# Four-head score groups, earlier-free accumulators in the opening, and moved value products in a two-layer decoder trunk

## The chip, the cores and the metric

The kernel runs on one core of one Trainium2 chip. The metric is the device time of one execution in microseconds (us); lower is better. Matrix products run on TensorE (PE in the profile), elementwise work on VectorE (DVE) and ScalarE (ACT), small powers on GpSimd (POOL); SyncE (SP) issues the loads. A weight load of TensorE is PEld.

## The reference, cut to what matters

A sequence of 256 positions of width 1024 goes through two layers. Layer A is a dilated sliding-window attention: three groups (window, dilation) = (128,1), (512,4), (2048,16), each with its own q, k and v of 16 heads of 64, merged by their softmax denominators. Layer B is causal attention over one block of 256. Each layer is followed by a gated ConvFFN of inner width 2816. All is float32.

```python
def reference(x, ...):
    for i in range(2):
        hn = rmsnorm(x, attn_norm[i])
        x = x + (mixer_dilated if i == 0 else mixer_moba)(hn, ...)   # qkv, q/k norm, rope, softmax, w_o
        hn = rmsnorm(x, ffn_norm[i])
        x = x + conv_ffn(hn, ffn_w_up[i], ffn_conv_w[i], ffn_conv_b[i], ffn_w_down[i])
    return x
```

## The kernel before, in words

Every weight matrix is streamed from HBM in units of 512 KB to 1 MB (`Stream`). ScalarE rounds a unit to its high part (`whi`, line 103), VectorE subtracts to get the low part (`wlo`, line 111), and TensorE makes each product from three multiplications (high by high, low by high, high by low; lines 428 to 430, 485 and 843 to 845).

The whole program is written out by hand as a sequence of turns. `turn` starts some weight units on ScalarE, runs what was put down for this turn in the list `first`, finishes one weight unit, runs the list `pre`, finishes the other units, issues a piece of a product on TensorE, and last runs the list `post`. Every engine works in the order in which the instructions are issued there. `at(post, 2, f)` puts f into the list of two turns later. In `post` the order is `step_C`, `step_A`, `step_T`, `transpose` (while the turn number is under 80).

Layer A works in four sections of four heads. A section's turns each hold 12 products of 512 columns. A section has four products for q and k of the three groups and for v (and in sections 0 and 2 one more for v), so it has 20, 16, 20 and 16 turns. After a q/k product come: squares and a copy out of the accumulator on ScalarE (lines 502, 503), sums and rotation on VectorE (`head_sums`, 508 to 520), a power on POOL, a scaling (`factors`, 530), and four TensorE transposes (`transpose`, 545), whose copies are lines 575 and 581 to 583. In the section's turn 14 and later the softmax steps follow, for one chunk of 128 queries (c) and some heads at a time:

- `step_A` (TensorE): scores of two heads side by side, three pairs of 64-row products with 256 columns (645), then for the dilated groups 16 products of 64 x 64 (654).
- `step_E` (VectorE, ScalarE): mask, maximum, exponential (667 to 677); `step_R`: division by the sum (684, 687).
- `step_T` (TensorE): transposes of the probabilities (694); `step_V` (ScalarE): copies out of PSUM (701).
- `step_C` (TensorE): value products, for all four heads and both chunks at once (725), and then `split_T` (416, 417).

PLANS gives the turns at which the groups of two heads stand in even and odd sections; a turn past the section's end falls into the next section. PSUM has eight banks: three for `acc`, two for `S`, two for `PT`, one for `O`. A pool gives out the buffer whose last use stands earliest in the program, and the first writer waits for that last use.

In section 0 the products of groups 0 and 1 (`both_chunks`) take one weight unit per turn and work on both chunks. `out_proj` is the output projection in pieces, each one weight unit by one chunk; OUT_ORDER gives their order. Layer B's mixer has the same steps with other sizes.

Of the kernel before, what the change touches and what calls it, by code (L numbers as in the profile page):

```python
# [44 lines left out]

PLANS = (14, 18, 24, 26), (14, 16, 22, 24)

# [88 lines left out]
def trunk_kernel(ctx, tc, x, a_w_qkv, a_w_o, b_w_qkv, b_w_o, ffn_norm, ffn_w_up, ffn_w_down, pack, mask_a, mask_b,  # L136
# [196 lines left out]
    class LateNorm(Norm):  # L333
# [20 lines left out]
        def transpose(self, h):  # L354
            xg = bp.tile([P, 512], F32, name="qk", bufs=4)
            t = self.flip(xr[:, self.c, h * 512:(h + 1) * 512], ("S", "PT")[self.c], 2)
            g = self.gain[:, h * 4:h * 4 + 4, None].to_broadcast([P, 4, P])
            nc.vector.tensor_mul(xg.rearrange("p (k t) -> p k t", t=P), t.rearrange("p (k t) -> p k t", t=P), g)
            split_T(self.dst, h * 4, 4, self.c, xg)

    class FirstNorm:
# [21 lines left out]
        def sums(self):  # L383
            acc = ps.tile([P, 512], F32, name="S", bufs=2)
# [48 lines left out]
    def attention(xT, norms, ng, g0, mask):  # L433
# [62 lines left out]
        def qk_block(sec, g, res, rq):  # L496
# [27 lines left out]
            def factors(c, qk, rs):  # L524

                h0 = 0 if dil else HS
                if not dil:
                    rq[c] = rs
                t3 = qk.rearrange("p (h d) -> p h d", d=HD)[:, h0:]
                nc.vector.tensor_mul(t3, t3, rs[:, h0:, None].to_broadcast([P, 8 - h0, HD]))  # L530
                at(post, 1, transpose, c, qk)

            def transpose(c, qk):
                if c == 0:
# [8 lines left out]
                tp = ps.tile([P, 512], F32, name="S", bufs=2) if dil and sec == 0 and g < 2 else new_acc()  # L543
                for i in range(4):
# [39 lines left out]

            yield from both_chunks(done) if dil and sec == 0 and g < 2 else product(done)

# [38 lines left out]

        O, weights = {}, {}

        def step_A(sec, c, heads, qkT, v, rq):

            S2 = [ps.tile([P, 512], F32, name="S", bufs=2) for _ in range(2)]  # L630
            n = 3 * P if dil else (c + 1) * P
            cs = slice(c * P, (c + 1) * P)

            for i in range(0, len(heads), 2):
                two = [(S2[h % 2], i // 2 * n, slice(h % 2 * HD, h % 2 * HD + HD), h // 2) for h in heads[i:i + 2]]
                if not dil and c == 0:
# [10 lines left out]
                if dil:  # L647
                    for a in range(2):
                        r = slice(a * 64, (a + 1) * 64)
                        for j in range(2):  # L650
                            t = qkT[1 + (a + j) % 2][c]
                            for s2, o, rows, pr in two:
                                oj = o + S + j * 64
                                nc.tensor.matmul(s2[r, oj:oj + 64], r32(t[rows, 0, pr, r]), r32(t[rows, 1, pr, r]),
                                                 start=True, stop=True)
            at(first, 1, step_E, sec, c, heads, v, rq, S2, n)

        def step_E(sec, c, heads, v, rq, S2, n):
            den = sp.tile([P, 4], F32, name="den", bufs=2)
            sm = bp.tile([P, 768], F32, name="sm", bufs=2)  # L660
            mx = sp.tile([P, 4], F32, name="mx", bufs=2)
            nb_ = sp.tile([P, 4], F32, name="nbias", bufs=2)

            m = len(heads)
            for i, h in enumerate(heads):
                o = i // 2 * n
                nc.vector.tensor_tensor_reduce(
                    out=sm[:, i * n:(i + 1) * n], in0=S2[h % 2][:, o:o + n], in1=mask[:, c * moff:c * moff + n],
                    op0=ALU.add, op1=ALU.max, scale=1.0, scalar=-3.0e38, accum_out=mx[:, i:i + 1])
            if dil:  # L670
                nc.vector.tensor_scalar_mul(nb_[:, 0:m], mx[:, 0:m], -1.0)
            else:
                f = rq[c][:, heads[0]:heads[0] + m]
                nc.vector.scalar_tensor_tensor(nb_[:, 0:m], mx[:, 0:m], -1.0, f, op0=ALU.mult, op1=ALU.mult)
            for i, h in enumerate(heads):
                sl = slice(i * n, (i + 1) * n)
                nc.scalar.activation(sm[:, sl], sm[:, sl], AF.Exp, bias=nb_[:, i:i + 1],
                                     scale=1.0 if dil else rq[c][:, h:h + 1], accum_out=den[:, i:i + 1])
            at(first, 1, step_R, heads, sm, den, n)
            at(post, 1 if dil or sec < NSEC - 1 else 2, step_T, sec, c, heads, v, sm, n)  # L680

        def step_R(heads, sm, den, n):
            rd = sp.tile([P, 4], F32, name="rd", bufs=2)
            nc.vector.reciprocal(rd[:, 0:len(heads)], den[:, 0:len(heads)])
            for i in range(len(heads)):
                sl = slice(i * n, (i + 1) * n)
                nc.vector.tensor_scalar(sm[:, sl], sm[:, sl], rd[:, i:i + 1], None, op0=ALU.mult)

        def step_T(sec, c, heads, v, sm, n):
            tot = n * len(heads)  # L690
            Tp = [ps.tile([P, 512], F32, name="PT", bufs=2) for _ in range((tot + 511) // 512)]
            for b in range(tot // P):
                o = b % 4 * P
                nc.tensor.transpose(Tp[b // 4][:, o:o + P], sm[:, b * P:(b + 1) * P], ident)  # L694
            at(pre, 1, step_V, sec, c, heads, v, Tp, tot)

        def step_V(sec, c, heads, v, Tp, tot):
            pT = bp.tile([P, 768], F32, name="pT", bufs=4)
            for i, t in enumerate(Tp):
                w = min(512, tot - i * 512)  # L700
                nc.scalar.activation(pT[:, i * 512:i * 512 + w], t[:, 0:w], AF.Copy)

# [3 lines left out]
            if heads[-1] < HS - 1 and (whole or not dil) or whole and c == 0:  # L706
                weights[key] = held
            else:
                at(post, 1, step_C, sec, held)

        def step_C(sec, held):

            for c, heads, pT, v in held:
# [4 lines left out]
                for i in range(0, len(heads), 2):  # L718
# [3 lines left out]
                    for n, (b, q, vb) in enumerate(blocks):  # L722
                        for j, h in enumerate(heads[i:i + 2]):
                            o, p = h // 2 * P, ((i + j) * nblk + b) * P
                            nc.tensor.matmul(O[sec, c][j * HD:(j + 1) * HD, c, o + q.start:o + q.stop],  # L725
                                             vb[:, h * HD:(h + 1) * HD], pT[:, p + q.start:p + q.stop],
                                             start=(n == 0), stop=(n == len(blocks) - 1))
# [10 lines left out]
        for sec in range(NSEC):  # L738
            qk, v, rq = [], vs[sec], {}
            for s, c, heads in last if sec == NSEC - 1 else odd if sec % 2 else plan:  # L740
                at(post, s, step_A, sec, c, heads, qk, v, rq)
# [9 lines left out]
    def out_proj(l, aT, dst):  # L751
# [4 lines left out]
        def piece(*idx):  # L756
            def go():
                for c, i in idx:
# [4 lines left out]
                    if u == 0:  # L763
                        acc[c, n] = ps.tile([P, 512], F32, name="S" if c and n else "acc", bufs=2 if c and n else 3)
                    for kk in range(2):
# [22 lines left out]
    def ffn(xT, l, end):  # L788
# [4 lines left out]

        st0 = [{"acc": ps.tile([P, 512], F32, name="PT", bufs=2)} for _ in range(2)]
        box = {}
# [103 lines left out]
        def down(b, c, ns=(0, 1), piece=None):  # L899
            f, e = divmod(b, 2)  # L900
            cs = slice(e * S + c * P, e * S + (c + 1) * P)
            if not dacc:
                dacc.extend([ps.tile([P, 512], F32, name=t, bufs=2) for _ in range(2)] for t in ("S", "PT"))
            if b not in dw:
# [69 lines left out]

    warm = ps.tile([P, 512], F32, name="PT", bufs=2)
    nc.scalar.activation(sp.tile([P, 512], F32, name="sq", bufs=2)[:, 0:P], ident, AF.Copy)
# [129 lines left out]
```

## Time and profile before

| | |
|---|---|
| median of 3 runs | 775.03 us (774.76 to 775.91) |
| the profiled execution: its time, its span | 775.08 us, 773.3 us |
| TensorE busy | 767.4 us (99%) |
| weight loads busy | 641.7 us (83%) |
| VectorE busy | 575.3 us (74%) |
| ScalarE busy | 497.5 us (64%) |
| HBM traffic | 172 GB/s over the span |

The span is the time from the first to the last instruction in the profile. The busy time of TensorE counts pipelined products whose ends are modelled, so that 99% busy does not say that each product takes as little time as it could; the distance from one start to the next does.

### The profile page before, as it was taken

To read this page: it belongs to the slowest core of one execution; us is meant where nothing else is said; L and a number is where in the kernel's file an instruction comes from. 1 tells how busy PE (TensorE), PEld (TensorE's weight loads), DVE (VectorE), ACT (ScalarE), POOL (GpSimd) and SP (SyncE) were. 2 spreads that over 40 slices of the span, in tenths; PEclk is the share of its full clock that TensorE was granted. 3 is DMA by queue.
4 is the path that set the end of the run, shared out by engine and by line. 5 is a ranking of instruction groups with operands and counts; after the bars stand their busy time and mean duration, and the time that the engine had idled before them with its cause. 6 is when DMAs were issued, how large, how long until landed. Compare 5 with 4: busy or idle time off the path is not lost.

```text
span 773.3 us, 12315 instructions
## 1 busy us (share of the span) xinstructions
PE 767.4 (99%) x4532; PEld 641.7 (83%) x4532; DVE 575.3 (74%) x1075; ACT 497.5 (64%) x867; POOL 84.1 (11%) x109
## 2 busy tenths in 40 slices
PE   8999999999999999999999999999999999999998
PEld 7878888888887789988888888787778988888886
DVE  6966767765786566878787786978866788877874
ACT  7768567567657556565666656868765566576560
POOL 1530331420232000000000002123000000000000
PEclk9999999999999999999999999999999999999999
DMA  9966536455546426556666563743526456656631
GB/s 285 326 189 182 156 110 191 137 164 164 158 151 207 141 81 206 177 183 198 195 208 197 166 217 107 231 151 109 183 90 201 153 181 197 212 172 190 197 103 54
DMA packets 108060, 133.84 MB, mean 173 GB/s; under 512 B 5856, under 2 KB 92768, under 8 KB 108000
## 3 DMA queue, kind: packets, MB, share of 16 engines
q1 hardware_dynamic: 107424, 130.96, 53.7%
q0 software_dynamic: 576, 2.10, 0.8%
q8 instruction: 35, 0.57, 0.3%
q14 instruction: 25, 0.20, 0.1%
HBM read 131.99 MB, written 1.05 MB: 172 GB/s over the span
## 4 chain that ended last, share of the span: by engine, by line
PE 92%; DVE 3%; ACT 1%; DMA 1%; issue 1%; SPq 0%; DVEq 0%; ACTq 0%
PE acc L428 12%; PE acc L430 12%; PE acc L429 12%; PE acc L843 12%; PE acc L845 6%; PE O L843 4%; PE S L909 3%; PE S L911 3%; PE S L910 3%; PE PT L909 3%; PE PT L911 3%; PE PT L910 3%; PE PT L694 2%; PE O L725 2%; PE acc L868 2%; PE acc L866 2%
## 5 line engine op out<-in xcount | busy, mean ns | idle before, releaser
L111 DVE TENSOR_TENSOR wlo<-raw,whi 128x1024 fp32r<-128x1024 f32 x240 | 287.7, 1220 | 6.5 <-ACT whi L103 6.3
L103 ACT ACTIVATE whi<-raw 128x1024 fp32r<-128x1024 f32 x240 | 244.9, 1053 | 5.1 <-DMA raw<-in_a_w_qkv_dram 2.2
L428 PE MATMUL acc<-whi,xT 128*128 128x512 f32 x432 | 175.2, 406 | 0.0
L430 PE MATMUL acc<-wlo,xT 128*128 128x512 f32 x432 | 169.0, 391 | 0.0
L429 PE MATMUL acc<-whi,xT 128*128 128x512 f32 x432 | 168.5, 390 | 0.1
L843 PE MATMUL acc<-xT,whi 128*128 128x512 f32 x384 | 137.3, 398 | 0.0
L845 PE MATMUL acc<-xT,wlo 128*128 128x256 f32 x384 | 107.8, 281 | 0.0
L430 PEld LDWEIGHTS acc<-wlo,xT 128*128 128x128 f32 x432 | 81.1, 188 | 17.9
L428 PEld LDWEIGHTS acc<-whi,xT 128*128 128x128 f32 x432 | 81.2, 188 | 16.5 <-issue 1.2
L429 PEld LDWEIGHTS acc<-whi,xT 128*128 128x128 f32 x432 | 81.4, 188 | 15.5 <-DVE xT L417 0.5
L843 PEld LDWEIGHTS acc<-xT,whi 128*128 128x128 f32 x384 | 72.1, 188 | 17.5
L845 PEld LDWEIGHTS acc<-xT,wlo 128*128 128x128 f32 x384 | 72.4, 189 | 1.2
L883 DVE SCALAR_TENSOR_TENSOR qk<-sm,pk,qk 128x254 f32<-128x254 f32 (+1 forms) x128 | 54.6, 478 | 4.0 <-ACT qk L880 3.1
L292 POOL TENSOR_TENSOR rs_y<-rs_v,mhalf 128x8 f32<-128x8 f32 x32 | 54.6, 1705 | 2.7
L855 DVE TENSOR_TENSOR sm<-acc,pT 128x256 f32<-128x256 f32 x48 | 20.3, 423 | 36.4 <-ACT pT L854 36.4
L880 ACT ACTIVATE qk<-sm,pk 128x256 f32<-128x256 f32 x64 | 38.3, 598 | 13.3 <-DVE sm L855 13.2
L843 PE MATMUL O<-xT,whi 128*128 128x512 f32 x128 | 46.1, 399 | 0.0
L892 ACT ACTIVATE kT<-qk 128x512 fp32r<-128x512 f32 x22 | 13.9, 633 | 47.7 <-DVE qk L890 47.7
L886 ACT ACTIVATE qk<-qk 128x512 f32<-128x512 f32 x22 | 13.9, 634 | 41.9 <-DVE qk L883 41.9
L290 POOL TENSOR_SCALAR rs_v<-qssq,rn_e 128x8 f32<-128x8 f32 x32 | 14.3, 446 | 212.8 <-DVE qssq L508 212.8
L866 PE MATMUL acc<-xT,whi 128*128 128x256 f32 x128 | 36.4, 284 | 0.0
L868 PE MATMUL acc<-xT,wlo 128*128 128x256 f32 x128 | 36.2, 283 | 0.0
(174 smaller groups left out, 1258.1 us busy)
## 6 DMA issues: line engine op xcount, KB each, us to landing
raw<-in_ffn_w_up_dram SPq DMA_DIRECT2D x80, 512.0 KB, 4.6
raw<-in_a_w_qkv_dram SPq DMA_DIRECT2D x144, 256.0 KB, 4.3
raw<-in_ffn_w_down_dram SPq DMA_DIRECT2D x44, 512.0 KB, 3.3
raw<-in_b_w_qkv_dram SPq DMA_DIRECT2D x48, 256.0 KB, 3.7
raw<-in_a_w_o_dram SPq DMA_DIRECT2D x8, 512.0 KB, 4.0
raw<-in_ffn_w_up_dram SPq DMA_DIRECT2D x16, 256.0 KB, 4.5
raw<-in_b_w_o_dram SPq DMA_DIRECT2D x8, 512.0 KB, 4.0
xr<-in_x_dram POOLq DMA_DIRECT2D x2, 512.0 KB, 6.0
```

Of the source, the lines that this page charges most:

```text
L103: self.nc.scalar.activation(hi, raw, AF.Copy)
L111: self.nc.vector.tensor_sub(lo, self.raw[self.done], r32(hi))
L292: nc.gpsimd.tensor_tensor(y, v, mhalf[:, 0:n], op=ALU.pow)
L428: nc.tensor.matmul(acc, T[:, k, 0, cs], hi, start=first, stop=False)
L429: nc.tensor.matmul(acc, T[:, k, 1, cs], hi, start=False, stop=False)
L430: nc.tensor.matmul(acc, T[:, k, 0, cs], lo, start=False, stop=last)
L843: nc.tensor.matmul(acc, hi[:, k % 4, es], xT[:, k].rearrange("p j t -> p (j t)"), start=(k == 0), stop=False)
L845: nc.tensor.matmul(acc[:, S:2 * S], lo[:, k % 4, es], xT[:, k, 0], start=False, stop=(k == 7))
L866: nc.tensor.matmul(o, hi[:, k % 4, es], xT[:, k, 0], start=(k == 0), stop=False)
L868: nc.tensor.matmul(o, lo[:, k % 4, es], xT[:, k, 0], start=False, stop=(k == 7))
L883: nc.vector.scalar_tensor_tensor(o[:, d:S], u[:, 0:S - d], cw[:, first_tap + b:first_tap + b + 1], o[:, d:S], op0=ALU.mult, op1=ALU.add)
L909: nc.tensor.matmul(o, acts[f][:, 0, cs], hi[:, sl], start=start, stop=False)
```

## The change

Scores of layer A's sections 0 to 2 are made for four heads at once, so that a section has two groups and not four. `step_A` then issues the 64-row products of both pairs, and after them all the 64 x 64 products; each head has a PSUM bank. `step_E` is run twice, for two heads each, the first time in `first`, the second in `pre`. The transposes come four turns after the scores, not two. Value products of sections 0, 1 and 2 are put down for turns 34, 50 and 69, which are turns in which scores of the next section stand. The pools `S` and `PT` become one pool `S` of four banks. In the opening, the second accumulator of group 1's product is the bank `O`, which is idle then, and the transposes of groups 0 and 1 stand one turn later. In layer B's output projection the first piece of chunk 1 stands between the pieces 3 and 4 of chunk 0.

```diff
-PLANS = (14, 18, 24, 26), (14, 16, 22, 24)
+PLANS = (14, 24), (14, 20)
+C_TURN = (34, 30, 33)
...
-             tuple((1, (0, u)) for u in range(8)) + tuple((int(u < 6), (1, u)) for u in range(8)))
+             ((1, (0, 0)), (1, (0, 1)), (1, (0, 2)), (1, (0, 3)), (1, (1, 0)), (1, (0, 4)), (1, (0, 5)), (1, (0, 6)), (1, (0, 7)), (1, (1, 1)),
+              (1, (1, 2)), (1, (1, 3)), (1, (1, 4)), (1, (1, 5)), (0, (1, 6)), (0, (1, 7))))
...
-        def both_chunks(done):
+        def both_chunks(done, first_block):
...
-                        accs.extend(new_acc() for _ in range(2))
+                        accs.extend((new_acc(), new_acc() if first_block else ps.tile([P, 512], F32, name="O", bufs=1)))
...
-                at(post, 1, transpose, c, qk)
+                at(post, 2 if dil and sec == 0 and g < 2 else 1, transpose, c, qk)
...
+            banks = [ps.tile([P, 512], F32, name="S", bufs=4) for _ in range(len(heads) if dil else 2)]
+            place = [(banks[i], 0) if dil else (banks[i % 2], i // 2 * n) for i in range(len(heads))]
+            todo = [(s2, o, slice(h % 2 * HD, h % 2 * HD + HD), h // 2) for (s2, o), h in zip(place, heads)]
+            pairs = [todo[i:i + 2] for i in range(0, len(heads), 2)]
+            for two in pairs:
...
+            for two in pairs if dil else ():
+                for a in range(2):
...
+            wide = dil and len(heads) > 2
+            for i in (0, 2) if wide else (0,):
+                at(pre if i else first, 1, step_E, c, heads, rq, place, n, slice(i, i + 2 if wide else len(heads)), sm, den, mx, nb_)
+            at(first, 2, step_R, heads, sm, den, n)
+            at(post, 4 if wide else 3 if not dil and sec == NSEC - 1 else 2, step_T, sec, c, heads, v, sm, n)
...
-            at(first, 1, step_R, heads, sm, den, n)
-            at(post, 1 if dil or sec < NSEC - 1 else 2, step_T, sec, c, heads, v, sm, n)
...
-            Tp = [ps.tile([P, 512], F32, name="PT", bufs=2) for _ in range((tot + 511) // 512)]
+            Tp = [ps.tile([P, 512], F32, name="S", bufs=4) for _ in range((tot + 511) // 512)]
...
-                at(post, 1, step_C, sec, held)
+                at(post, starts[sec] + C_TURN[sec] - now[0] if whole and dil else 1, step_C, sec, held)
...
-            plan, odd = ([(s, i // 2, (i % 2 * 2, i % 2 * 2 + 1)) for i, s in enumerate(p)] for p in PLANS)
+            plan, odd = ([(s, c, (0, 1, 2, 3)) for c, s in enumerate(p)] for p in PLANS)
```

All other tiles that were named `S` with two buffers or `PT` are now `S` with four; probabilities of four heads take two `sm` and two `pT` tiles.

## Rows read from the trace of the kernel before

**Rows 1.** The page's first part: busy time of each engine.
```profile
PE 767.4 (99%) x4532; PEld 641.7 (83%) x4532; DVE 575.3 (74%) x1075; ACT 497.5 (64%) x867; POOL 84.1 (11%) x109
```

**Rows 2.** Waits of TensorE: engine, tile, line <- releaser: total us, times, longest.
```profile
PE acc L485 <- ACT qk L503: 0.6, 1, 0.6
```

**Rows 3.** Timeline of TensorE around one score group: start us, us, engine, line, operation.
```profile
83.18 0.39 PE L430 MATMUL acc<-wlo,xT 128*128 128x512 f32 x1
83.50 0.62 PE L645 MATMUL S<-kT 64*128 64x256 f32 x6
84.05 0.47 PE L654 MATMUL S<-t 64*64 64x64 f32 x16
...
84.87 0.47 PE L428 MATMUL acc<-whi,xT 128*128 128x512 f32 x1
85.18 0.39 PE L429 MATMUL acc<-whi,xT 128*128 128x512 f32 x1
```

**Rows 4.** The same group, cut after four and after twelve products.
```profile
83.50 0.50 PE L645 MATMUL S<-kT 64*128 64x256 f32 x4
...
84.05 0.42 PE L654 MATMUL S<-t 64*64 64x64 f32 x12
```

**Rows 5.** Timeline of TensorE where four transposes stand alone between products.
```profile
45.91 0.39 PE L430 MATMUL acc<-wlo,xT 128*128 128x512 f32 x1
46.14 0.60 PE L545 MATMUL acc<-ident,qk 128*128 128x128 f32 x4
46.50 0.48 PE L428 MATMUL acc<-whi,xT 128*128 128x512 f32 x1
```

**Rows 6.** Timeline of TensorE at the start of section 0's value products.
```profile
104.47 0.39 PE L430 MATMUL acc<-wlo,xT 128*128 128x512 f32 x1
104.78 2.90 PE L725 MATMUL O<-pT,v 128*64 128x128 f32 x64
```

**Rows 7.** Timeline of TensorE in the opening, two stretches.
```profile
18.42 0.48 PE L485 MATMUL acc<-whi,xT 128*128 128x512 f32 x1
...
20.25 0.62 PE L485 MATMUL acc<-wlo,xT 128*128 128x512 f32 x2
...
39.14 0.39 PE L430 MATMUL acc<-wlo,xT 128*128 128x512 f32 x1
39.71 0.63 PE L545 MATMUL S<-ident,qk 128*128 128x128 f32 x4 [0.18 <-DVE qk L530]
```

**Rows 8.** Timeline of TensorE in layer B's output projection.
```profile
566.50 0.40 PE L428 MATMUL acc<-whi,xT 128*128 128x512 f32 x1
566.95 0.50 PE L429 MATMUL acc<-whi,xT 128*128 128x512 f32 x1
```

**Rows 9.** Timeline of VectorE: opening, a softmax group, a division.
```profile
17.30 1.22 DVE L111 TENSOR_TENSOR wlo<-raw,whi 128x1024 fp32r<-128x1024 f32 x1
...
43.76 0.68 DVE L530 TENSOR_TENSOR qk<-qk,rs_y 128x512 f32<-128x512 f32 x1
...
85.81 0.54 DVE L667 CUSTOM_DVE_ANT_0 sm<-S,mA 128x384 f32<-128x384 f32 x1
...
87.68 1.22 DVE L111 TENSOR_TENSOR wlo<-raw,whi 128x1024 fp32r<-128x1024 f32 x1
...
125.46 0.75 DVE L687 TENSOR_SCALAR sm<-sm,rd 128x384 f32<-128x384 f32 x2
```

**Rows 10.** Timeline of ScalarE: accumulator copy, split of value products, turn 35.
```profile
88.77 0.58 ACT L503 ACTIVATE qk<-acc 128x512 f32<-128x512 f32 x1
...
112.15 0.63 ACT L416 ACTIVATE xT<-O 128x256 fp32r<-128x256 f32 x1 [0.69 <-DVE xT L417]
...
122.03 1.99 ACT L103 ACTIVATE whi<-raw 128x1024 fp32r<-128x1024 f32 x2
123.93 0.60 ACT L677 ACTIVATE sm<-sm,nbias 128x384 f32<-128x384 f32 x1
```

**Rows 11.** Timeline of TensorE: the first product of turn 35.
```profile
120.98 0.47 PE L428 MATMUL acc<-whi,xT 128*128 128x512 f32 x1
```

More of the change, by code (lines that the diff above doesn't have):

```diff
@@ L383, in sums @@
         def sums(self):
-            acc = ps.tile([P, 512], F32, name="S", bufs=2)
+            acc = ps.tile([P, 512], F32, name="S", bufs=4)
             for c in range(2):
@@ L542, in transpose @@
                                   bp.tile([P, 2, 2, S], F32R, name="kT", bufs=QB))
-                tp = ps.tile([P, 512], F32, name="S", bufs=2) if dil and sec == 0 and g < 2 else new_acc()
+                tp = ps.tile([P, 512], F32, name="S", bufs=4) if dil and sec == 0 and g < 2 else new_acc()
                 for i in range(4):
@@ L583, in second_parts @@
                         nc.vector.scalar_tensor_tensor(lo, src, scale, r32(hi), op0=ALU.mult, op1=ALU.subtract)
-            yield from both_chunks(done) if dil and sec == 0 and g < 2 else product(done)
+            yield from both_chunks(done, g == 0) if dil and sec == 0 and g < 2 else product(done)
         def new_v():
@@ L624, in v_last @@
             yield from product(done)
-        O, weights = {}, {}
+        O, weights, starts = {}, {}, []
         def step_A(sec, c, heads, qkT, v, rq):
-            S2 = [ps.tile([P, 512], F32, name="S", bufs=2) for _ in range(2)]
             n = 3 * P if dil else (c + 1) * P
             cs = slice(c * P, (c + 1) * P)
-            for i in range(0, len(heads), 2):
-                two = [(S2[h % 2], i // 2 * n, slice(h % 2 * HD, h % 2 * HD + HD), h // 2) for h in heads[i:i + 2]]
+            banks = [ps.tile([P, 512], F32, name="S", bufs=4) for _ in range(len(heads) if dil else 2)]
[3 more added lines that the diff above has]
+            for two in pairs:
                 if not dil and c == 0:
@@ L646, in step_A @@
                                          start=(a + b == 0), stop=(b == 1))
[L647 to L666, printed above, removed]
+            for two in pairs if dil else ():
+                for a in range(2):
+                    r = slice(a * 64, (a + 1) * 64)
+                    for j in range(2):
+                        t = qkT[1 + (a + j) % 2][c]
+                        for s2, o, rows, pr in two:
+                            oj = o + S + j * 64
+                            nc.tensor.matmul(s2[r, oj:oj + 64], r32(t[rows, 0, pr, r]), r32(t[rows, 1, pr, r]),
+                                             start=True, stop=True)
@@ new lines, in step_A @@
+            den, mx, nb_ = (sp.tile([P, 4], F32, name=t, bufs=2) for t in ("den", "mx", "nbias"))
+            sm = []
+            wide = dil and len(heads) > 2
[3 more added lines that the diff above has]
+            at(post, 4 if wide else 3 if not dil and sec == NSEC - 1 else 2, step_T, sec, c, heads, v, sm, n)
@@ L667, in step_E @@
+        def step_E(c, heads, rq, place, n, part, sm, den, mx, nb_):
+            t = bp.tile([P, 768], F32, name="sm", bufs=2)
+            these = range(len(heads))[part]
+            sm.extend(t[:, i * n:(i + 1) * n] for i in range(len(these)))
+            for i in these:
+                s2, o = place[i]
                 nc.vector.tensor_tensor_reduce(
-                    out=sm[:, i * n:(i + 1) * n], in0=S2[h % 2][:, o:o + n], in1=mask[:, c * moff:c * moff + n],
+                    out=sm[i], in0=s2[:, o:o + n], in1=mask[:, c * moff:c * moff + n],
@@ L669, in step_E @@
                     op0=ALU.add, op1=ALU.max, scale=1.0, scalar=-3.0e38, accum_out=mx[:, i:i + 1])
             if dil:
-                nc.vector.tensor_scalar_mul(nb_[:, 0:m], mx[:, 0:m], -1.0)
+                nc.vector.tensor_scalar_mul(nb_[:, part], mx[:, part], -1.0)
             else:
[L673 to L678, printed above, removed]
@@ L679, in step_E @@
-            at(first, 1, step_R, heads, sm, den, n)
-            at(post, 1 if dil or sec < NSEC - 1 else 2, step_T, sec, c, heads, v, sm, n)
+                f = rq[c][:, heads[these[0]]:heads[these[-1]] + 1]
+                nc.vector.scalar_tensor_tensor(nb_[:, part], mx[:, part], -1.0, f, op0=ALU.mult, op1=ALU.mult)
+            for i in these:
+                nc.scalar.activation(sm[i], sm[i], AF.Exp, bias=nb_[:, i:i + 1],
+                                     scale=1.0 if dil else rq[c][:, heads[i]:heads[i] + 1], accum_out=den[:, i:i + 1])
@@ L739, in attention @@
             qk, v, rq = [], vs[sec], {}
+            starts.append(now[0])
             for s, c, heads in last if sec == NSEC - 1 else odd if sec % 2 else plan:
@@ L763, in go @@
                     if u == 0:
-                        acc[c, n] = ps.tile([P, 512], F32, name="S" if c and n else "acc", bufs=2 if c and n else 3)
+                        acc[c, n] = ps.tile([P, 512], F32, name="S" if c and n else "acc", bufs=4 if c and n else 3)
                     for kk in range(2):
@@ L791, in ffn @@
         acts, dw = {}, {}
-        st0 = [{"acc": ps.tile([P, 512], F32, name="PT", bufs=2)} for _ in range(2)]
+        st0 = [{"acc": ps.tile([P, 512], F32, name="S", bufs=4)} for _ in range(2)]
         box = {}
@@ L902, in down @@
             if not dacc:
-                dacc.extend([ps.tile([P, 512], F32, name=t, bufs=2) for _ in range(2)] for t in ("S", "PT"))
+                dacc.extend([ps.tile([P, 512], F32, name="S", bufs=4) for _ in range(2)] for _ in range(2))
             if b not in dw:
```

23 lines of the change are left out of this document (12 added, 11 removed).

## The prediction

> **What bounds the kernel now.** I read the page's first part, then the waits of TensorE, and last TensorE's timeline around the steps that change. The page shows TensorE busy for 767.4 of 773.3 us, with VectorE and ScalarE at three quarters and below [rows 1]. The view of waits has hardly anything for TensorE: its longest wait after the first products is 0.6 us, in the opening, for a copy on ScalarE [rows 2]. So TensorE sets the time nearly everywhere, and an edit is worth what it takes out of TensorE's own queue. Busy time does not tell that, since the ends of pipelined products are modelled; the distance between starts does. In the timeline a product of 512 columns is followed by the next work after 0.23 us (45.91 to 46.14 [rows 5]), and small work between two products shows as a longer distance. VectorE and ScalarE matter only where they would make TensorE wait.
>
> **Merging the score groups (largest term).** From the last product before a two-head group to the first one behind it pass 1.69 us (83.18 to 84.87 [rows 3]); the four transposes that stand in the same turn take 0.59 us when they are alone (45.91 to 46.50 [rows 5]). So a group adds 1.10 us. A four-head group has three more pairs of 64-row products. Cut after four products, the row lasts 0.50 us, with all six 0.62 [rows 3, 4]: 0.12 a pair, 0.36 for three. It has sixteen more 64 x 64 products; the last four of sixteen add 0.05 (0.42 to 0.47 [rows 3, 4]), so 0.20. It thus adds 1.10 + 0.36 + 0.20 = 1.66 us, against 2.20 for two groups: 0.54 saved. Sections 0, 1 and 2 each lose two groups, so 6 x 0.54 = 3.2 us. The reason is to be seen in the rows: the three pairs take 0.55 us from their first start to the next shape (83.50 to 84.05 [rows 3]) where three steps of 0.12 would be 0.36, so the first pair after a change of shape is dear, and so is the way in (83.18 to 83.50, 0.32 against 0.23 [rows 3, 5]). The number of transposes of probabilities and of value products stays, and they cost what they did.
>
> No row shows four heads in one group. The least saving would be that the second pair of heads pays all starts again and only the ways in and out are saved: 0.09 for the way in, and about half of the 0.26 us by which the rest of the group (84.05 to 84.87, 0.82) exceeds four fours of 0.05 and the transposes' 0.36 [rows 3 to 5]; that is 0.22 each, 1.3 us in all. I take 3.2, since the pairs and fours inside the present group already have different weights each and yet follow at 0.12 and 0.05.
>
> **Value products beside scores.** Alone, the value products start 0.31 us behind a product (104.47 to 104.78 [rows 6]) and not 0.23, and what follows starts late by as little. Put in front of a score group of the next section, one way in and one way out are saved: 0.1 us each, three times, 0.3. No row has value products next to scores. If nothing at all were lost between the two, it would be 0.2 each and 0.6; if the change between them cost twice, nothing. The Trainium skill's page "TensorEngine Tiling (Array Packing)", section "Key Properties", says that a change of the tiling mode drains TensorE. By that rule the change from 128 x 64 to 64 x 128 tiles still drains once, and the sum would take 0.3 and not 0.6; the trace's dear first pairs agree with it.
>
> **The opening.** Group 1's first matmul starts at 18.42, the fifth (the first with low weights) at 20.25: 1.83 us [rows 7]. Without a wait it would be 0.31 for the first distance after small work (84.87 to 85.18 [rows 3]) and three of 0.23, 1.00 us. The wait is for the copy that frees the accumulator [rows 2]; with bank `O` the second accumulator is free, so 0.83 us are saved. What is late next would be the low weights: they are done at 17.30 + 1.22 = 18.52 [rows 9], and TensorE would want them at 19.42. The second loss is at 39.14, from where the transposes take 0.57 us to start instead of 0.23, waiting for the scaling on VectorE [rows 7]; one turn later that scaling is long done, 0.34 saved. Together 1.2 us. The transposes' copies and subtractions move one turn later too, in the queues of ScalarE and VectorE; group 2's scaling stands behind them, and it ends at 43.76 + 0.68 = 44.44 [rows 9]. TensorE reaches its transposes at 46.14 now [rows 5] and would at 44.9: 0.5 us of cover. If VectorE were the limit here, up to the whole 1.2 would be lost.
>
> **The independent output projection piece.** At 566.50 two products of layer B's projection are 0.45 us apart, not 0.23 [rows 8]: the second reads the low part of the last heads' outputs, just made. A piece of chunk 1 ahead of it is six products of 0.23, 1.4 us of cover. I take 0.2; nothing at the least, 0.3 at the most.
>
> **What the change may add.** The pool `S` gives all four banks to one group. VectorE has read them after four reads of 0.54 us [rows 9], and the next user, the transposes, comes four turns later. A turn is 12 x 0.23 = 2.8 us, so this costs nothing. The tightest chain is that of the groups with value products in front (turns 34 and 50). In turn 35 TensorE starts at 120.98 [rows 11]; ScalarE does two weight roundings from 122.03 to 124.02, and now the exponentials follow [rows 10]. After the change the two splits stand between: copy 0.63, wait 0.69, copy 0.63 [rows 10], then a subtraction of some 0.65, to 126.6. Four reads and two negations on VectorE take 2.4, to 129.0, the last two exponentials 1.2 more (0.60 each [rows 10]), to 130.2, and four divisions with the reciprocal 1.7 (0.75 for two [rows 9]), to 131.9. TensorE wants the probabilities after four turns, at 120.98 + 11.0 = 132.0, and those of the last two heads 0.6 later. So it is hidden, with 0.7 us to spare where it ends last. The other groups have no split in front and more room. I take 0.
>
> **Sum.** 3.2 + 0.3 + 1.2 + 0.2 = 4.9 us off the profiled execution's 775.08, 770.2; its span would go from 773.3 to 768.4. The median of the runs is 0.05 below that execution, so 770.1 is forecast for the median.
>
> **Rivals.** First, slower: TensorE waits for accumulators behind the four-head softmax. In the groups at a section's turn 4, the second half of `step_E` stands on VectorE behind a weight subtraction that ends at 88.90 [rows 9]. Its reads and negation take 1.2, its exponentials 1.2, and only then come the square and the copy that free the q/k accumulator, 1.1: 92.4, where it is 89.35 now [rows 10]. The next transposes but one would start at 84.87 + 0.56 + two turns = 91.0 [rows 3]. If they got that bank, each of the three places would cost 1.4 us. At turns 38 and 54 the copies of v come in the same way behind the splits and all four exponentials: they would end at 130.2 + 1.4 = 131.6, where a product three turns after 120.98 wants a bank at 129.3, 2.3 each. Together 3 x 1.4 + 2 x 2.3 = 8.8, less 4.9: 3.9 slower, 778.9. It decides for slower from 1 us at each of the five places on. Against it: a pool gives out the buffer that the program has left longest; that is the bank of the short-lived transposes, and the product's own bank comes up a turn or more later, at 94.2 for the first kind. The Trainium skill's same page, section "Performance Considerations", warns of this in general: packing speeds up TensorE and not the copies out of PSUM, which may become the limit; by it these waits would be the likely outcome. The trace so far has one such wait, of 0.6 us [rows 2].
>
> Second, the merged groups keep the cost of their starts: 1.3 and not 3.2, so 772.0. For it speaks only that no row has such a group. Third, the opening gives nothing, because VectorE's queue holds TensorE a few turns later: 771.3. Fourth, the change does not do what it says in sum: several small new waits (0.5 to 1 us at each group) eat what the shorter groups give, and the time stays near 775.
>
> **Chances.** The forecast 0.70; merged groups that save little 0.08; opening lost 0.08; no change 0.06; slower by accumulators 0.08. A measurement of this kernel can tell about 0.2%, 1.55 us, from no change: the first three cases are faster than 773.5, so faster 0.86, same 0.06, slower 0.08. The range starts at 769.3, where the value products save 0.6, the projection 0.3 and the six groups some 0.07 more each, and ends at 772.6, above the second and third rival; it leaves out the two cases at 775 and 778.9 and a little of the others.
>
> **What would show it.** Groups of line 645 with 12 products that reach line 654's 32 in 0.91 us and the next transposes 0.6 us later; the value products starting at scores' side; the opening's distance of 1.83 near 1.0 and no wait for line 503; the pair at 566.50 at 0.23; TensorE busy some 5 us less. Wrong would be: TensorE waits for lines 503, 598 or 601 behind exponentials, waits of the transposes (694) for line 687, or a first pair of 0.2 us in the middle of a group.

## The result

The changed kernel takes 771.16 us (median of 4 runs, 770.46 to 771.70) against 775.08 us (774.76 to 775.91) for the kernel before on the same chip: a ratio of 0.9947, 95% interval 0.993 to 0.9965. That is 3.9 us faster, where 4.9 was forecast. The four times lie two and two, 770.46 and 770.67, 771.65 and 771.70; the last is the profiled execution, with a span of 769.9.

The page's first part and the view of TensorE's waits, for the changed kernel (waits: engine, tile, line <- releaser: total us, times, longest). Its lines from 90 on are numbered 3 to 9 higher than before.

```profile
PE 763.3 (99%) x4532; PEld 642.3 (83%) x4532; DVE 573.4 (74%) x1069; ACT 496.7 (65%) x867; POOL 88.8 (12%) x109
```
```profile
PE acc L548 <- DVE qk L533: 1.2, 1, 1.2
PE acc L488 <- ACT whi L93: 0.5, 1, 0.5
```

TensorE is busy 4.1 us less than in [rows 1]. The wait of [rows 2] is gone. A new one is there: four q/k transposes wait 1.2 us for the scaling on VectorE. The 0.5 us is one product of the first turns behind the first weights; it comes and goes from run to run (0 to 1.1 us in the profiles below).

TensorE's timeline in the opening, around a merged score group, and in layer B's output projection:

```profile
18.57 0.49 PE L488 MATMUL acc<-whi,xT 128*128 128x512 f32 x1
18.90 0.40 PE L488 MATMUL O<-whi,xT 128*128 128x512 f32 x1
...
19.60 0.39 PE L488 MATMUL acc<-wlo,xT 128*128 128x512 f32 x1
...
81.48 0.39 PE L433 MATMUL acc<-wlo,xT 128*128 128x512 f32 x1
81.80 0.97 PE L650 MATMUL S<-kT 64*128 64x256 f32 x12
82.70 0.74 PE L659 MATMUL S<-t 64*64 64x64 f32 x32
83.37 0.66 PE L548 MATMUL acc<-ident,qk 128*128 128x128 f32 x4
83.78 0.47 PE L431 MATMUL acc<-whi,xT 128*128 128x512 f32 x1
...
563.40 0.39 PE L431 MATMUL acc<-whi,xT 128*128 128x512 f32 x1
563.63 0.40 PE L432 MATMUL acc<-whi,xT 128*128 128x512 f32 x1
```

From the first product of group 1 to the first with low weights pass 1.03 us (18.57 to 19.60) instead of 1.83 [rows 7]. Four heads' scores reach the 64 x 64 products after 0.90 us (0.91 foretold), and these last 0.67 to the next transposes (about 0.6 foretold). Without the transposes' 0.59 the group adds 2.30 - 0.59 = 1.71 us (81.48 to 83.78), where two groups of the kernel before add 2.20 [rows 3, 5] and 1.66 was foretold. The pair in the projection is 0.23 us apart, not 0.45 [rows 8].

Where the time went is seen best from the first product of each turn, after against before, in the two profiled executions. Turn 4 itself starts between 0.34 us earlier and 0.47 us later than before in the profiles of this document, with the first loads, so gains are counted from turn 4 or later:

| stretch | start of turns, after minus before | change | foretold |
|---|---|---|---|
| opening, turns 4 to 13 | +0.16 to -1.06 us | -1.22 | -1.2 |
| turns 13 to 73, without the loss in turns 43 and 44 | | -3.67 | -3.5 |
| loss in turns 43 and 44 | | +1.67 | 0 |
| from there to the output projection | -3.06 to -3.11 | -0.05 | 0 |
| order of the projection | -3.11 to -3.42 | -0.31 | -0.2 |

(From turn 13 to 73 the difference goes from -1.06 to -3.06, that is -2.00; the loss is what this kernel loses there against the run with the value products put back, below.) So every saving came in at its size or a little over, and one place that was foretold at nothing took 1.7 us. The four engines there (timelines of the changed kernel; TensorE, GpSimd, VectorE, ScalarE):

```profile
147.61 0.39 PE L433 MATMUL acc<-wlo,xT 128*128 128x512 f32 x1
147.98 0.50 PE L431 MATMUL acc<-whi,xT 128*128 128x512 f32 x1
148.32 0.40 PE L432 MATMUL acc<-whi,xT 128*128 128x512 f32 x1
...
150.84 1.47 PE L700 MATMUL S<-ident,sm 128*128 128x128 f32 x12
153.51 0.63 PE L548 MATMUL acc<-ident,qk 128*128 128x128 f32 x4 [1.20 <-DVE qk L533]
```
```profile
149.91 2.73 POOL L295 TENSOR_TENSOR rs_y<-rs_v,mhalf 128x8 f32<-128x8 f32 x1
```
```profile
149.92 1.22 DVE L114 TENSOR_TENSOR wlo<-raw,whi 128x1024 fp32r<-128x1024 f32 x1
152.67 0.69 DVE L533 TENSOR_TENSOR qk<-qk,rs_y 128x512 f32<-128x512 f32 x1 [1.53 <-POOL rs_y L295]
```
```profile
146.27 0.60 ACT L685 ACTIVATE sm<-sm,nbias 128x384 f32<-128x384 f32 x1
...
147.35 0.58 ACT L506 ACTIVATE qk<-acc 128x512 f32<-128x512 f32 x1
```

Read from the end: the transposes at 153.51 wait for the scaling at 152.67, the scaling waits for a power on GpSimd, and the power took 2.73 us. Most of these powers take 1.64 to 1.68. It began 18 ns before VectorE's weight subtraction, which ran its usual 1.22 us; the power's extra 1.09 us is nearly that. A second, smaller loss has no idle time in the records: the product at 147.98 is 0.37 us behind its forerunner, and the next again 0.34, not 0.23 each (0.25 lost). It starts 0.05 us after a copy out of an accumulator has ended (147.35 + 0.58 = 147.93), which stood behind the exponentials.

### The profile page after: what moved, and what is told of

It is laid out like the page before. It is cut to its first block, busy times and chain, and to the rows that moved or that the text cites. A ratio compares the mean times of both kernels' runs of the same rounds, so it can differ in the third digit from the quotient of the medians.

```text
span 769.9 us, 12315 instructions
## 1 busy us (share of the span) xinstructions
PE 763.3 (99%) x4532; PEld 642.3 (83%) x4532; DVE 573.4 (74%) x1069; ACT 496.7 (65%) x867; POOL 88.8 (12%) x109
## 4 chain that ended last, share of the span: by engine, by line
PE 92%; DVE 3%; ACT 2%; DMA 1%; issue 1%; POOL 0%; SPq 0%; DVEq 0%; ACTq 0%
PE acc L851 12%; PE acc L431 12%; PE acc L433 11%; PE acc L432 11%; PE acc L853 6%; PE S L917 5%; PE S L919 5%; PE S L918 5%; PE O L851 4%; PE O L732 2%; PE acc L876 2%; PE acc L875 2%; PE acc L874 2%; PE O L853 2%; PE acc L488 2%; PE S L700 2%
## 5 line engine op out<-in xcount | busy, mean ns | idle before, releaser
L853 PE MATMUL acc<-xT,wlo 128*128 128x256 f32 x384 | 107.8, 281 | 0.0
L917 PE MATMUL S<-whi,kT 128*128 128x512 f32 x174 | 68.5, 394 | 0.0
L919 PE MATMUL S<-wlo,kT 128*128 128x512 f32 x174 | 68.0, 391 | 0.0
L918 PE MATMUL S<-whi,kT 128*128 128x512 f32 x174 | 67.8, 390 | 0.0
L295 POOL TENSOR_TENSOR rs_y<-rs_v,mhalf 128x8 f32<-128x8 f32 x32 | 58.8, 1839 | 2.7
```

What stands on the lines that cost most here:

```text
L295: nc.gpsimd.tensor_tensor(y, v, mhalf[:, 0:n], op=ALU.pow)
L853: nc.tensor.matmul(acc[:, S:2 * S], lo[:, k % 4, es], xT[:, k, 0], start=False, stop=(k == 7))
L917: nc.tensor.matmul(o, acts[f][:, 0, cs], hi[:, sl], start=start, stop=False)
L918: nc.tensor.matmul(o, acts[f][:, 1, cs], hi[:, sl], start=False, stop=False)
L919: nc.tensor.matmul(o, acts[f][:, 0, cs], lo[:, sl], start=False, stop=stop)
```

## The experiments

All were timed against the kernel before, whose median was 774.95 to 775.01 us. "Turn 44" is the turn of the new wait. The unedited changed kernel was run again as well (further down). Its times spread over 1.4 us, which has to be kept in mind for the first two experiments.

**Is it the late scaling?** The four transposes stand one turn later (late44).

```diff
-                at(post, 2 if dil and sec == 0 and g < 2 else 1, transpose, c, qk)
+                at(post, 2 if dil and (sec == 0 and g < 2 or (sec, g, c) == (2, 1, 0)) else 1, transpose, c, qk)
```


> One product's transposes (section 2, group 1, chunk 0) stand one turn later than in the changed kernel; nothing else differs. In the changed kernel's trace they wait 1.2 us for the scaling of q and k, which waits for a power on POOL. If that wait is a loss of TensorE's own time, it goes, with the slow restart behind it: 1.4 us off the profiled execution, a median of about 769.9 against 771.2. If TensorE would only wait for the same thing somewhere later, the time stays at 771.

770.44 us (769.86 to 770.65), ratio 0.9941 (0.9928 to 0.9953), 0.5 over the number expected. The wait is gone from the profile, and from turn 4 on the profile gains 1.40 us on the changed kernel's; the product behind the late copy (0.35 us behind its forerunner, then 0.33) stays. But the power took only 1.64 us in this profile. With such a power the unedited kernel has no wait here either (its second profile, below), and against that profile the edit gains 0.27 us. The median is that of the unedited kernel when it was run again. So this run shows that the transposes can stand later, not that the edit saves 1.4 us.

**Is it the subtraction beside the power?** A small VectorE instruction on a few numbers stands in front, so that the weight subtraction starts later (gap). It writes a tile that nothing reads.

```diff
                 nc.vector.tensor_add(t4[:, :, :, 0:16], ra, rb)
+                gap = sp.tile([P, 2], F32, name="gap", bufs=1)
+                nc.vector.tensor_scalar_mul(gap, ssq[:, 0:2], -1.0)
```


> A tiny VectorE instruction (two numbers per partition, one input) stands between the rotation's last addition and the weight subtraction that follows it, in each of the 32 places; the computed values do not change. Theory: the power on POOL (1.64 to 1.70 us as a rule) takes 2.73 us where the subtraction, which reads two operands from SBUF, starts within some 20 ns of it and gets ahead; with the gap the subtraction starts 100 ns or more after it, every power lasts at most 1.70 us, the wait of 1.2 us shrinks to about 0.2, and the median is about 770.2. Rival: the power is late for its own reasons, or because any subtraction runs beside it; then some powers still take 2.7 us and the time stays at 771, or a little above for the added instructions.

770.67 us (770.45 to 771.29), ratio 0.9946 (0.9934 to 0.9959). Here the subtraction starts 137 ns after the power, the power takes 1.64 us, and the wait falls from 1.2 to 0.2 us. None of the 32 powers of this size is long in this profile (at most 1.70 us); no subtraction starts less than 87 ns after one. In turn 12 this profile also loses 0.4 us that the others don't, so the wait says more here than the time:

```profile
PE acc L550 <- DVE qk L535: 0.2, 1, 0.2
```

So the power's extra 1.1 us made most of the wait; but even a short power comes a little late. Something had pushed the whole queue back.

**What pushed it?** The value products go back to their old place (c_back).

```diff
-                at(post, starts[sec] + C_TURN[sec] - now[0] if whole and dil else 1, step_C, sec, held)
+                at(post, 1, step_C, sec, held)
```


> The value products of sections 0 to 2 stand one turn behind the last copy of the probabilities again (turns 30, 46, 66), alone between products; the rest is as in the changed kernel. By the forecast's term each costs 0.1 us more, 0.3 in all; by the changed kernel's trace, where the two turns with scores and value products are about 0.14 shorter than the sum, 0.4. So 771.5. If the position is worth nothing for TensorE, 771.2. If the long chain of splits and exponentials behind them cost the changed kernel something, the time falls under 771.

769.76 us (769.69 to 769.99), ratio 0.9934 (0.9921 to 0.9948): faster than the changed kernel. Of the expectation's three cases it is the last, for which no number was given; that the moved value products only gain is refuted. TensorE's queue does lose 0.13 to 0.14 us at each of two places, as expected, and turn 44 gives back the whole 1.67 us. The power there starts at 147.66, 2.25 us earlier than in the changed kernel, while the turn starts only 0.55 us earlier. It took 1.64 us in this profile, but a long one would have been in time as well, by an estimate from these rows: 147.66 + 2.73 and 0.69 for the scaling make 151.08, and the transposes start at 151.46. The cause stands nine turns ahead, at turn 35. ScalarE's timeline there, first in the changed kernel and then with the value products put back:

```profile
122.16 0.61 ACT L419 ACTIVATE xT<-O 128x256 fp32r<-128x256 f32 x1
123.44 0.62 ACT L419 ACTIVATE xT<-O 128x256 fp32r<-128x256 f32 x1 [0.68 <-DVE xT L420]
125.89 0.62 ACT L685 ACTIVATE sm<-sm,nbias 128x384 f32<-128x384 f32 x1 [1.82 <-DVE nbias L680]
...
129.63 1.06 ACT L106 ACTIVATE whi<-raw 128x1024 fp32r<-128x1024 f32 x1
```
```profile
121.80 0.60 ACT L685 ACTIVATE sm<-sm,nbias 128x384 f32<-128x384 f32 x1
...
125.52 1.07 ACT L106 ACTIVATE whi<-raw 128x1024 fp32r<-128x1024 f32 x1
```

The two splits in front of the softmax cost 1.23 us of copies, and ScalarE stands still twice, 0.68 and 1.82 us, while VectorE subtracts and then reads the scores (these reads stand behind the subtractions in its queue). Together that is 3.7 of the 4.1 us by which the next rounding is later (129.63 against 125.52; TensorE's turn 35 starts only 0.36 us later). At turn 44 about 1.8 us of it is left.

**Is it the splits or the value products?** The value products stay beside the scores, and the splits of sections 0 and 1 go to the end of the turn two later (split_late).

```diff
-                    at(first, 1, split_T, aT, sec * 2, 2, c, O[sec, c][:, c], dil)
+                    at(*(post, 2) if dil and sec < 2 else (first, 1), split_T, aT, sec * 2, 2, c, O[sec, c][:, c], dil)
```


> The changed kernel, but the two splits of sections 0 and 1's value products stand at the end of the turn two later, behind the four-head softmax and its divisions. Theory: the value products beside the scores cost nothing themselves (each saves 0.14 us of TensorE against the old place); what costs is that the split's two copies and two subtractions stand in front of the softmax, so that VectorE and ScalarE wait for each other and run 4.1 us later at turn 38 and 1.8 us later at turn 44, where TensorE then waits 1.2 us for the scaling (line 533). By it the wait at turn 44 goes, the 0.2 us at that turn's start (a product behind the copy of line 506) too, and the time is some 1.5 us under the changed kernel and 0.4 us under the run with the value products put back: 769.3 us, span 767.5. Rival: any work of a value product in a score turn delays the softmax by as much wherever its split stands (TensorE's own order does it): then the wait at turn 44 stays and the time is 771.0 us.

769.86 us (769.77 to 770.31), ratio 0.9934 (0.9921 to 0.9948). The exponentials start at 122.01, right behind the roundings, and turn 44 has no wait. So it is the splits' place. The time is 0.6 over the number expected, and no better than with the value products put back.

Three kernels were then run side by side on one chip: the changed kernel with no edit, the late splits, and the value products put back.

> The changed kernel once more, unedited, on the chip of the next two. Theory: its times fall on two levels some 1.1 us apart, near 770.5 and 771.6 us, as the power on GpSimd at turn 44 takes 1.64 or 2.73 us; the profiled execution's level goes with that power's duration in its trace. Rival: the spread is that of the first loads and has nothing to do with the power: then the level goes with the start of the first product (5.4 to 6.1 us) and the power's duration does not matter.

> The late splits once more, beside the two others on one chip. Theory: 0.3 us under the run with the value products put back (two places at 0.14 us and the third at 0.14 less the 0.11 it gives back at turn 73, so 0.2 to 0.4), both 0.7 to 1.8 us under the changed kernel. Rival: no difference between the two, since the value products beside the scores save too little to outlast what moves with them.

> The value products put back once more, beside the two others on one chip: 769.8 us by the earlier run, narrow (0.3 us from lowest to highest), since no wait stands at turn 44 whatever the power's duration there. If its times spread over 1 us as the changed kernel's do, the spread is not the power's.

| run | median of 5, us | lowest to highest | ratio, 95% |
|---|---|---|---|
| changed kernel | 770.44 | 770.28 to 771.65 | 0.9945 (0.9932 to 0.9957) |
| late splits | 769.89 | 769.63 to 770.18 | 0.9935 (0.9921 to 0.9948) |
| value products put back | 770.04 | 769.76 to 770.14 | 0.9935 (0.9922 to 0.9947) |

No time of the two edited kernels reaches those of the changed kernel. They are 0.4 to 0.6 us shorter on the medians, less than the 0.7 expected at the least.

The profile of the unedited changed kernel caught the other outcome (GpSimd, VectorE, TensorE):

```profile
149.60 1.64 POOL L295 TENSOR_TENSOR rs_y<-rs_v,mhalf 128x8 f32<-128x8 f32 x1
```
```profile
149.62 1.26 DVE L114 TENSOR_TENSOR wlo<-raw,whi 128x1024 fp32r<-128x1024 f32 x1
151.27 0.69 DVE L533 TENSOR_TENSOR qk<-qk,rs_y 128x512 f32<-128x512 f32 x1 [0.39 <-POOL rs_y L295]
```
```profile
150.53 1.47 PE L700 MATMUL S<-ident,sm 128*128 128x128 f32 x12
152.11 0.63 PE L548 MATMUL acc<-ident,qk 128*128 128x128 f32 x4
```

Same code, and turn 45 starts 1.10 us earlier against turn 44 than in the first profile; all else agrees to 0.03 us but the start, which is 0.28 us earlier at turn 4. So the power makes 1.1 of the 1.4 us between the two executions and the first loads 0.3. The execution with the long power took 771.70 us, this one 770.28. The nine timed runs of the changed kernel lie between 770.28 and 770.67 (five) and between 771.12 and 771.70 (four), the ten with the value products put back within 0.5 us. That the other runs' levels are this power's too is likely, but only the two profiled executions show it.

From turn 4 on, the profiles with the late splits gain 0.26 and 0.20 us on those with the value products put back, near the 0.3 expected. That is too little for the timed runs to tell.

**How much of the merging lies in the order inside the group?** Four heads per group, but each pair does its 64-row products and its 64 x 64 products before the next pair starts (pairwise).

```diff
-            for two in pairs if dil else ():
-                for a in range(2):
...
+                for a in range(2 if dil else 0):
```


> Groups of four heads as in the changed kernel, but each pair's 64-row products are followed by that pair's 64 x 64 products, so that the shape changes three times more in each group; same products, other order. If the first products after a change of shape are what a group's start costs, each of the six groups takes 0.37 us longer (0.54 + 0.41 once more for the second pair, against 0.34 + 0.23), 2.2 us in all, 773.4. If the saving of the merged groups lies in the ways in and out alone, the time stays at 771.2.

772.47 us (771.90 to 774.57, 6 runs), ratio 0.9975 (0.9963 to 0.9986). TensorE's timeline of the same group:

```profile
82.46 0.62 PE L650 MATMUL S<-kT 64*128 64x256 f32 x6
83.01 0.47 PE L658 MATMUL S<-t 64*64 64x64 f32 x16
83.41 0.62 PE L650 MATMUL S<-kT 64*128 64x256 f32 x6
83.96 0.47 PE L658 MATMUL S<-t 64*64 64x64 f32 x16
84.37 0.66 PE L548 MATMUL acc<-ident,qk 128*128 128x128 f32 x4
```

From the first score to the transposes pass 1.91 us instead of 1.57 (81.80 to 83.37), 0.34 more, and the turns' starts show the same 0.33 to 0.34 at each of the six groups: 2.0 us, where 2.2 was expected. The second pair pays its starts again, as the prediction's least case had it. The time rose by less, 1.3 us between the medians, since the long wait at turn 44 is absent in this profile. Two of its six runs took 774.5 us; their mean granted clock, 0.999 and 1.000, is no lower than the profiled run's 0.999, so the clock is not the reason, and the reason stays open.

**What is the merging worth in all?** Groups of two heads at the turns of the kernel before, everything else changed (two_heads).

```diff
-PLANS = (14, 24), (14, 20)
+PLANS = (14, 18, 24, 26), (14, 16, 22, 24)
...
-            plan, odd = ([(s, c, (0, 1, 2, 3)) for c, s in enumerate(p)] for p in PLANS)
+            plan, odd = ([(s, i // 2, (i % 2 * 2, i % 2 * 2 + 1)) for i, s in enumerate(p)] for p in PLANS)
```


> The changed kernel with groups of two heads at the turns of the kernel before, all else as changed. Theory: the merging is worth 3.2 us of TensorE (six times 0.54), and the wait at turn 44 (1.5 us) goes too, since no four-head softmax stands behind a split there: 771.2 + 3.2 - 1.5 = 772.9 us, span 771.3. Rival: the merging saves 1.3 us only and the rest of the gain came from the other edits: 771.0 us. Third: the wait at turn 44 does not hang on the merged groups: 774.4 us.

780.15 us (779.95 to 782.66), ratio 1.0074 (1.0061 to 1.0086): slower than the kernel before, which none of the three cases expected. The view of waits says why:

```profile
PE S L700 <- DVE sm L692: 5.1, 2, 3.0
```

Groups of two heads have their transposes two turns after the scores. At turns 36 and 52 these now wait for divisions that stand behind the splits. Turns 35 to 38 lose 3.7 us against the kernel before and turns 51 to 53 3.2. That is 6.9 us for 5.1 us of waiting, and most of the rest is TensorE's clock. Its timeline after the first wait:

```profile
128.25 0.85 PE L700 MATMUL S<-ident,sm 128*128 128x128 f32 x6 [2.09 <-DVE sm L692]
128.86 0.68 PE L431 MATMUL acc<-whi,xT 128*128 128x512 f32 x1
129.33 0.63 PE L432 MATMUL acc<-whi,xT 128*128 128x512 f32 x1
129.76 0.63 PE L433 MATMUL acc<-wlo,xT 128*128 128x512 f32 x1
```

After the 2.09 us of idle time the granted clock was 0.50 from 129.0 to 132.0, the lower of the two levels (1.2 GHz, not 2.4), and the products follow at 0.43 us instead of 0.23. Eight distances, from 128.86 to 132.32, lose 1.5 us by that. After the second wait, 2.96 us, the clock stayed at 1.00. The mean granted clock of the five timed runs goes with their times: 0.997 to 0.998 at 779.95 to 780.15 us, 0.995 at 781.20, 0.993 at 782.66.

With the two losses taken off, the gain from turn 13 to turn 73 is 0.26 us, near the value products' 0.3. The changed kernel gains 2.00 there, and 3.67 without its own 1.67, so the merging is worth some 3.4 us. The moved value products need the four turns that came with the merging.

**How much of the four turns is needed?** Transposes three turns after the scores (t_three).

```diff
-            at(post, 4 if wide else 3 if not dil and sec == NSEC - 1 else 2, step_T, sec, c, heads, v, sm, n)
+            at(post, 3 if wide else 3 if not dil and sec == NSEC - 1 else 2, step_T, sec, c, heads, v, sm, n)
```


> The changed kernel with the transposes of probabilities three turns behind the scores, not four. Theory (the prediction's chain): in the groups with value products in front the first division ends 9.9 us after the next turn's start, and three turns and the place in the turn give TensorE 8.3 us, so TensorE waits some 1.6 us at turns 37 and 53 for the divisions (line 692); the other groups have room. The wait at turn 44 goes, since TensorE is later by then: 771.2 - 1.5 + 3.2 = 772.9 us. Rival: the softmax has far more room than that chain says and a turn less costs nothing: 771.2 us or, with the wait at turn 44 gone, 769.7.

773.28 us (773.06 to 773.68), ratio 0.9978 (0.9969 to 0.9988), 0.4 over the expectation. The waits are those foretold, two of about 1.6 us, and no other is left at turn 44:

```profile
PE S L700 <- DVE sm L692: 3.1, 2, 1.5
```

**Opening and projection order alone**, on the kernel before (open_order).

```diff
-                        accs.extend(new_acc() for _ in range(2))
+                        accs.extend((new_acc(), new_acc() if first_block else ps.tile([P, 512], F32, name="O", bufs=1)))
...
-                at(post, 1, transpose, c, qk)
+                at(post, 2 if dil and sec == 0 and g < 2 else 1, transpose, c, qk)
...
+             ((1, (0, 0)), (1, (0, 1)), (1, (0, 2)), (1, (0, 3)), (1, (1, 0)), (1, (0, 4)), (1, (0, 5)), (1, (0, 6)), (1, (0, 7)), (1, (1, 1)),
...
```


> The kernel before with two edits alone: the opening (second accumulator in bank O, transposes of groups 0 and 1 one turn later) and the order of the output projection's pieces. Theory: 1.2 + 0.3 = 1.5 us off, 773.5 us; in the profile no wait for line 503, the distance from the first to the fifth product of turn 4 1.0 us, the product pair at the end of layer B's output projection 0.23 us apart. Rival: VectorE's queue gives the opening's gain back some turns later, so that little of it is left at turn 30: 774.7 us.

773.42 us (773.08 to 773.80, 11 runs), ratio 0.9979 (0.997 to 0.9988), as expected. In the turns' starts it gains 1.22 us from turn 4 to turn 13, 0.04 more by turn 82, and 0.32 at the projection: the opening's gain is not given back.

The shortest medians of all, 769.76 to 770.04 us, are those of the kernels without splits in front of the softmax. They beat the changed kernel by 0.4 to 0.6 us on the chip where both ran.

## Why the prediction was right, and where it was 1 us off

**Merging.** Foretold 3.2 us. From turn 13 to 73 the run with two-head groups puts it at 3.4, and the run with the value products put back gains 3.4 more than the run of opening and order alone. The rows of one group give 6 x (2.20 - 1.71) = 2.9 of it; the first distance behind small work, 0.31 us and not 0.23 [rows 3], is not in them and occurs less often now. The reason given, that starts after a change of shape are dear, is shown for the larger part: 2.0 us return when the pairs change shape once more. By subtraction some 1.4 us are left for the ways in and out, near the 1.3 of the prediction's least case; no run takes them apart. The second rival is out.

**Value products.** Foretold 0.3. In TensorE's queue two places save 0.14 us each and the third little (0.11 of its 0.14 is lost again at turn 73). What the foretold sum left out is what the move does to the other engines, below.

**Opening and projection.** Foretold 1.2 and 0.2, measured 1.22 and 0.31. The third rival is out.

**The step that failed** is the last of "What the change may add": "The other groups have no split in front and more room. I take 0." The chain it had costed was right. The last division ends 10.85 us after turn 35's first product, 10.9 foretold, and the transposes start at 11.0 without a wait (VectorE, then TensorE; the second row shows nine of the twelve transposes):

```profile
128.64 1.41 DVE L692 TENSOR_SCALAR sm<-sm,rd 128x384 f32<-128x384 f32 x4
```
```profile
130.22 1.14 PE L700 MATMUL S<-ident,sm 128*128 128x128 f32 x9
```

But a chain that is just hidden leaves its engines late. VectorE and ScalarE were 4.1 us behind at turn 38 and still 1.8 at turn 44, where the next four-head group had no split in front and yet no room. There the lateness costs 0.55 us (0.25 of it the product behind the late copy, the rest the four transposes, which start late even after a short power) and, when the power on GpSimd is the long one, 1.67. With 0.55 to 1.67 in place of 0, the foretold 4.9 becomes 4.4 to 3.2; measured are 4.6 and 3.9 on the medians of the two chips. The prediction knew nothing of the two lengths of the power, and which of them a run gets is chance as far as these runs show.

**The first rival** named the right kind of place, an accumulator behind the four-head softmax, at some 1.4 to 2.3 us five times. It was found once, at 0.25 us. The Trainium skill's page "TensorEngine Tiling (Array Packing)", section "Performance Considerations", says that copies out of PSUM may become the limit; in this case that is seen at turn 44 alone, by those 0.25 us, and there the copy was late because of the splits.

## What to carry to other kernels

When work is put in front of a chain on engines that have spare time, it is not enough that this chain still ends in time: follow how late it leaves each engine's queue until an idle stretch has taken it up, and look at the tightest wait on the way. A two-engine step (copy, then subtract) in front of another (read, then exponential) costs the handoffs as well as the work, and behind it the work may cost nothing. Edits may carry one another: with the moved value products TensorE waits 5.1 us where two-head groups have their transposes two turns behind the scores, 3.1 where four-head groups have them three turns behind, and not at all right there with four.

## What the runs showed of the hardware

The same 128 x 8 power on GpSimd takes 1.64 or 2.73 us, and a few nanoseconds go with the difference. Over ten profiles of the changed kernel and its variants (all but the one with the small instruction in front) VectorE's weight subtraction, which has two inputs in SBUF, starts 14 to 25 ns after such a power 98 times. At 14 to 18 ns the power is always the long one (13 of 13, 2.73 to 2.77 us) and the subtraction takes 1.22 us. At 21 to 25 ns the power always takes 1.64 to 1.68, and the subtraction 1.25 to 1.27. At 19 and 20 ns both occur. From 96 ns on, the power takes at most 1.70 and the subtraction 1.21 to 1.23.

The Trainium skill's page "SBUF — State Buffer", section "Who interferes with whom", says that a VectorE instruction with two inputs in SBUF contends with a GpSimd instruction that reads SBUF for a shared pair of ports, which the one that issues first holds for its whole length. The size of the loss agrees with that: the long power takes 1.1 us more beside a subtraction of 1.22. Two things in the traces do not. The power starts first in all 98 cases and is still the one that loses in the close ones; and a subtraction that starts 21 to 25 ns after a power loses only 0.04 us, one from 96 ns on nothing, where the whole length of a power would be 1.6. Why some nanoseconds decide, no run here tests.

TensorE's granted clock fell to 0.50 for 3 us after one idle time of 2.09 us, and not after one of 2.96 us, both in the run with two-head groups; at the lower level products of 512 columns follow at 0.43 us, at the higher at 0.23.
